# One pool for the weight buffers, stores issued by ScalarE, and later bias-table and cache loads in a streaming-encoder kernel

## Chip, cores and metric

The kernel runs on one core of one Trainium2 chip. The metric is device time in microseconds (us) of one execution; lower is better. The engines are called PE (TensorE matmul), PEld (its weight load), DVE (VectorE), ACT (ScalarE), POOL (GpSimd) and SP (SyncE); SPq and POOLq are the instruction queues of SP and POOL from which DMAs are issued.

## What is computed

One layer for 640 tokens (512 of a prompt, 128 new ones of eight streams), as five tiles of 128 tokens, width 2048. In short form:

```
z            = rmsnorm(x) @ w_in                   # q, k, v, u, vs, ga, gb
h            = sigmoid(ga) * (attention(q, k, v) @ w_pa)
             + sigmoid(gb) * (sgu(u, rmsnorm(gelu(vs))) @ w_pb)
x            = x + h @ w_out
q            = rmsnorm(x) @ w_query                # 8 heads, two half keys each
pick 16 of the 128*128 experts per head: scores sv, indices eidx, g = softmax(scores)
a            = gelu(expert_u[eidx] . rmsnorm(x))
y            = rmsnorm(x + sum((g * a) * expert_v[eidx]))
```

Attention is a sliding window with a bias table (`rel_bias_table`, by bucket of the distance) and, for the sampled tile, cached keys and values. Inputs and outputs are fp32.

## The kernel before

**Matrix products.** Every large product goes through `gemm` (L192). For two steps of 128 along the contraction it loads one `raw` tile (512 KB, L198); for each step ACT casts it to `whi` (fp32r, L143) and DVE makes the remainder `wlo` (L144; every `pl`-th one goes to POOL in some stages). For each token tile `i` PE then runs three matmuls, L211, L212 and L213 (whi with xh, wlo with xh, whi with xl), into one `acc` bank. Below, a **k-step** is this group for all token tiles of the stage: nine matmuls where there are three.

**Stages.** Two tiles (0 and the sampled one) go through `prep`, `mix` and `query` first, then the other three (1, 2, 3). For those three, the experts are computed densely (`dense_peer`, L802): `U` runs twelve gemms of x with the expert rows ("U loop", about 1750 to 2206 us in the trace), then sixteen rounds of `V` and the later `U` follow ("d stage", to the end). For tiles 0 and SAMPLE, single expert rows are gathered in the background (L754, used by DVE at L740 and L745).

**Weights of the experts.** Alongside the U loop, `weights` (L774) builds for each of the three tiles a matrix `wd` in DRAM in 32 steps: DVE and ACT make one-hot tiles `s` (L789, L795; ACT L792, L793), PE multiplies them (L796), ACT copies the result out of PSUM (L798), SP stores 256 KB (L799). `h_step` (L807) loads `wd` back into a `b` tile (L99), DVE multiplies it with the activation (L814), PE transposes it (L818), and ACT and DVE split it into `HT`, which `V` uses as its left side. `late(s)` is an `h_step` whose activation `ad` was stored by `U` (L831) and is loaded again. `late(0)` and `late(1)` are queued while the U loop still runs; each handles the three tiles one after the other.

**Order.** The side work sits in a list of generators (`side`), of which `gemm` runs one step every so often (`pump`). From this the Tile framework makes a fixed order of instructions for each engine; an engine runs its own list strictly in order, and waits on semaphores. SP issues nearly all loads and stores.

**Buffers.** The pools `wk` (work tiles: `s`, `S`, `e`, `b`) and `st` (`raw`, `whi`, `wlo`) are opened by `open_work`. After the U loop `work.close()` closes both, and they are opened again with other counts for the d stage (L863 to L868):

```python
                work.close()
                cfg.update(s=12, S=D_STAGE, b=D_LOAD, raw=D_RAW, w=D_W)
                open_work("d")
```

`whi` and `wlo` have N_W = 5 buffers each up to there and D_W = 6 in the d stage; `raw` has 4 in both, `b` 4 in both. A tile of the new pools waits for the old tiles that lay in its memory.

**Start.** `bias_table` (L219) multiplies the bias table with a one-hot matrix (L228) and stores the product 32 times over (768 KB) to DRAM as `bvd` (L231); it is the first generator in `side`. `start` is the generator that loads and splits the first two tiles' x (L426). `sample_consts` (L312) loads the caches.

Of the kernel before, what the change touches and what calls it, by code (L numbers as in the profile page):

```python
# [37 lines left out]
N_LOAD = 4  # L38
N_STAGE = 6
N_W = 5  # L40
D_W = 6
D_RAW = 4
D_STAGE = 5
D_LOAD = 4
N_RAW = 4
# [14 lines left out]
def body(tc, A, O):  # L60
    nc = tc.nc
    with ExitStack() as ctx:
# [6 lines left out]

        cfg = dict(s=N_SLOT, e=N_EV, b=N_LOAD, S=N_STAGE, raw=N_RAW, w=N_W)  # L70
        work = ExitStack()
        pools = {}

        def open_work(name):
            pools["wk"] = work.enter_context(tc.tile_pool(name="wk" + name, bufs=1, reuse_waits="tile"))
            pools["st"] = work.enter_context(tc.tile_pool(name="st" + name, bufs=1, reuse_waits="tile"))

        open_work("a")
        uid = [0]

        def nm(s):
            uid[0] += 1
            return f"{s}_{uid[0]}"

        def mtile(shape, dt=F32):
            return mt.tile(shape, dt, name=nm("m"), tag="m")

        def slot(shape=(128, 512), dt=F32):
            return pools["wk"].tile(list(shape), dt, name=nm("s"), tag="s", bufs=cfg["s"])

        def stage(shape=(128, 512), dt=F32):
            return pools["wk"].tile(list(shape), dt, name=nm("S"), tag="S", bufs=cfg["S"])

        def evs(shape=(128, 512)):
            return pools["wk"].tile(list(shape), F32, name=nm("e"), tag="e", bufs=cfg["e"])
# [9 lines left out]
        def misc(shape=(128, 512)):  # L105
            return pm.tile(list(shape), F32, name=nm("pm"), tag="pm")
# [23 lines left out]
        def stat(w=1):  # L130
            nstat[0] += w
            assert nstat[0] <= 208
            return stats[:, nstat[0] - w:nstat[0]]
# [41 lines left out]
        side = []  # L175
# [46 lines left out]
        def bias_table():  # L222
            tab = evs((32, 16))
            nc.sync.dma_start(tab, A["table"])
            oh = evs((32, 384))
            nc.sync.dma_start(oh, A["onehot"])
            p = misc()
            nc.tensor.matmul(p[:16, :384], tab, oh, start=True, stop=True)  # L228
            bv = evs((16, 384))
            nc.vector.tensor_copy(bv, p[:16, :384])  # L230
            nc.sync.dma_start(bvd, bv.unsqueeze(1).to_broadcast([16, 32, 384]))  # L231
            for _ in range(5):
                yield


# [76 lines left out]
        def sample_consts(vnat, out):  # L312
            vnd = dr.tile([128, 128], F32, name="vnd")
            nc.sync.dma_start(vnd, vnat)
            yield
            kc = mtile([128, 2, 8, 128])
            nc.vector.memset(kc, 0.0)
            for kv in range(2):
                nc.sync.dma_start(kc[kv * 64:kv * 64 + 64, kv], A["kcT"][kv * 64:kv * 64 + 64])
            vc = mtile([128, 8, 128])  # L320
            nc.sync.dma_start(vc, A["vc"])
            sk = stat(2)
            nc.sync.dma_start(sk, A["sinks_s"])
            bias = slot((128, 2, 144))
            for kv in range(2):
                nc.sync.dma_start(bias[:, kv, :],
                                  bass.AP(tensor=bvd.tensor, offset=bvd.offset + kv * 8 * 32 * 384 + 127,
                                          ap=[[32 * 384, 8], [383, 16], [1, 144]]))
            vn = mtile([16, 8, 128])
            nc.sync.dma_start(vn, vnd.rearrange("(b t) d -> t b d", b=8))  # L330
            out.extend((kc, vc, vn, sk, bias))
            yield

# [439 lines left out]
        wd = {}  # L773

        def weights(ti, ijg):
            wd[ti] = dr.tile([128, 16384], F32, name=nm("wd"))
            pt = misc((128, 4, 128))
            for c in range(3):
                nc.tensor.transpose(pt[:, c, :], ijg[:, c, :], ident)
            tr = stage((128, 4, 128))  # L780
            nc.scalar.copy(tr[:, 0:3, :], pt[:, 0:3, :])
            nc.vector.tensor_scalar_mul(tr[:, 3, :], tr[:, 1, :], -1.0)  # L782
            for t0 in range(0, 128, 4):
                pw = misc((128, 4, 128))
                for t in range(t0, t0 + 4):
                    if t % 2 == 0:
                        ab = slot((128, 4, 128))
                    a, b = ab[:, t % 2 * 2, :], ab[:, t % 2 * 2 + 1, :]
                    nc.vector.tensor_scalar(a, io128, tr[:, 0, t:t + 1], tr[:, 2, t:t + 1],  # L789
                                            op0=ALU.is_equal, op1=ALU.mult)  # L790
                    if t % 4 < ACT_OH:
                        nc.scalar.activation(b, io128, AF.Abs, bias=tr[:, 3, t:t + 1])  # L792
                        nc.scalar.activation(b, b, AF.Relu, bias=1.0, scale=-1.0)  # L793
                    else:
                        nc.vector.tensor_scalar(b, io128, tr[:, 1, t:t + 1], None, op0=ALU.is_equal)  # L795
                    nc.tensor.matmul(pw[:, t - t0, :], a, b, start=True, stop=True)  # L796
                w = slot((128, 4, 128))
                nc.scalar.copy(w, pw)  # L798
                nc.sync.dma_start(wd[ti][t0:t0 + 4, :].rearrange("t (i j) -> i t j", i=128), w)  # L799
                yield  # L800

        def dense_peer(G, x2T, r2, x1d):  # L802
            n = len(G)
            ad = [[dr.tile([128, 512], F32, name=nm("ad")) for _ in G] for _ in range(LEAD)]
            if True:
# [17 lines left out]
                def abuf():  # L823
                    return stage()

                def U(s, ticks):
                    def ev(i, ps):
                        a = abuf()
                        nc.scalar.activation(a, ps, AF.Gelu_apprx_tanh, scale=r2[i])
                        if s < LEAD:  # L830
                            nc.sync.dma_start(ad[s][i], a)  # L831
                        else:
                            side.append(h_step(s, i, a))
                    gemm(x2T, 0, KC, A["UT"][s], ev, ticks)
# [29 lines left out]
                drain()  # L864
                pl[0] = 0
                work.close()
                cfg.update(s=12, S=D_STAGE, b=D_LOAD, raw=D_RAW, w=D_W)
                open_work("d")  # L868
                steps[0] = 1.0
                for b in range(16):  # L870
# [3 lines left out]
                    for nb in range(4):  # L874
                        s = 2 * b + 2 + nb // 2
# [9 lines left out]
                for c in range(4):  # L885
                    cs = slice(c * 512, c * 512 + 512)
                    for i, ti in enumerate(G):
                        t = y[i, c]
# [8 lines left out]
        start = prep(G1, x1a, r1a, [(i, c) for c in range(4) for i in range(2)])  # L897
        next(start)
        next(start)
        side.append(bias_table())  # L900

        def start_rows(kc):
            if kc % 2 == 0 and kc:
                next(start)
                next(start)
            if kc == 6:
                side.insert(0, start)

        nextg = prep(G2, x1b, r1b, [(i, c) for i in range(3) for c in range(4)])

# [103 lines left out]
```

## Time and profile before

| what | value |
|---|---|
| median of 3 runs | 3988.98 us (3987.25 to 3996.61) |
| profiled execution, its own time | 3996.57 us |
| span of the profiled execution | 3994.9 us |
| PE busy | 3883.8 us, 97% of the span |
| DVE busy | 3153.5 us, 79% |
| ACT busy | 1728.2 us, 43% |
| POOL busy | 829.1 us, 21% |
| mean DMA rate | 296 GB/s |

The span is the time from the first to the last instruction in the trace; the execution's own time is 1.67 us longer. Busy time of an engine leaves out DMA-issuing instructions and waits. The granted clock is TensorE's, as a share of its full level.

### The profile page before, as it was taken

The numbers are of one execution on the slowest core, as the hardware profiler recorded it, in microseconds if no ns is written. First come the engines' busy times: TensorE is split into PE (matmuls) and PEld (weight loads), VectorE is DVE, ScalarE is ACT, GpSimd is POOL, SyncE is SP. The second block draws the span as 40 slices with busy tenths as digits, with TensorE's granted clock in tenths as the row PEclk, the third lists the DMA queues.
The fourth block names the chain that finished last, engine by engine and source line by source line (L and its number), as shares of the span: only waits on it lengthen the run. The fifth ranks groups of instructions, "written<-read, shape, count | busy, mean of one in ns | idle before, by whom it ended". The sixth has DMA issues, their size and how long they took to land. (4 is left out here: it accounts for less than half of the span.)

```text
span 3994.9 us, 52665 instructions
## 1 busy us (share of the span) xinstructions
PE 3883.8 (97%) x17880; PEld 3177.5 (80%) x17880; DVE 3153.5 (79%) x5421; ACT 1728.2 (43%) x3338; POOL 829.1 (21%) x678
## 2 busy tenths in 40 slices
PE   8999998999999999999999899999999999999998
PEld 6778786877777888877878788877888888888886
DVE  4655769966767987899977688878888888888888
ACT  5665554444444334436665333333333333333333
POOL 1000113211212223211111112222222222222222
PEclk9999999999999999999999999999999999999999
DMA  7666786777878997569988989989998999999987
GB/s 224 204 187 208 248 264 201 273 276 279 311 277 286 336 334 249 206 198 314 327 264 288 338 325 338 342 299 365 338 350 336 353 331 345 345 340 349 346 337 290
DMA packets 333919, 1180.51 MB, mean 296 GB/s; under 512 B 35840, under 2 KB 94784, under 8 KB 267088
## 3 DMA queue, kind: packets, MB, share of 16 engines
q1 hardware_dynamic: 259824, 640.15, 47.9%
q0 software_dynamic: 73824, 536.99, 35.0%
q8 instruction: 141, 2.31, 0.2%
q14 instruction: 130, 1.06, 0.1%
HBM read 1117.69 MB, written 59.31 MB: 295 GB/s over the span
## 5 line engine op out<-in xcount | busy, mean ns | idle before, releaser
L211 PE MATMUL acc<-whi,m 128*128 128x512 f32 (+1 forms) x5232 | 2066.7, 395 | 23.3 <-ACT whi L143 18.3
L212 PE MATMUL acc<-wlo,m 128*128 128x512 f32 (+1 forms) x5232 | 2049.8, 392 | 22.5 <-DVE wlo L144 22.4
L213 PE MATMUL acc<-whi,m 128*128 128x512 f32 (+1 forms) x5232 | 2044.1, 391 | 0.3 <-DVE m L144 0.2
L143 ACT CAST whi<-raw 128x512 fp32r<-128x512 f32 (+1 forms) x1888 | 1157.9, 617 | 1979.3 <-PE acc L213 1646.6
L144 DVE TENSOR_TENSOR wlo<-raw,whi 128x512 fp32r<-128x512 f32 (+1 forms) x1824 | 1221.5, 689 | 526.8 <-ACT whi L143 523.1
L212 PEld LDWEIGHTS acc<-wlo,m 128*128 128x128 f32 x5232 | 990.7, 189 | 227.1 <-DVE wlo L144 34.5
L211 PEld LDWEIGHTS acc<-whi,m 128*128 128x128 f32 x5232 | 989.3, 189 | 225.4 <-ACT whi L143 20.6
L213 PEld LDWEIGHTS acc<-whi,m 128*128 128x128 f32 x5232 | 989.5, 189 | 202.7 <-DVE m L144 0.8
L740 DVE SCALAR_TENSOR_TENSOR gb<-gb,xa 128x2048 f32<-128x2048 f32 x256 | 589.6, 2303 | 79.5 <-DMA gb<-in_U,idx 69.1
L745 DVE SCALAR_TENSOR_TENSOR xa<-gb,hw,xa 128x2048 f32<-128x2048 f32 x239 | 560.3, 2344 | 70.4 <-DMA gb<-in_V,idx 64.1
L754 POOL DMA_INDIRECT gb<-in_V,idx x239 | 318.5, 1333 | 1228.8 <-DVE wlo L144 331.2
L754 POOL DMA_INDIRECT gb<-in_U,idx x256 | 339.6, 1327 | 1018.9 <-ACT whi L143 366.2
L144 POOL TENSOR_TENSOR wlo<-raw,whi 128x512 fp32r<-128x512 f32 x64 | 91.5, 1431 | 261.8 <-ACT whi L143 229.7
L796 PEld LDWEIGHTS pm<-s 128*128 128x128 f32 x768 | 102.6, 193 | 30.5 <-ACT s L793 14.6
L796 PE MATMUL pm<-s 128*128 128x128 f32 x768 | 113.7, 283 | 10.0 <-DVE s L789 8.0
L789 DVE TENSOR_SCALAR s<-io,S 128x128 f32<-128x128 f32 x384 | 114.8, 339 | 3.6 <-DMA wd<-s 3.6
L847 DVE TENSOR_TENSOR s<-s,acc 128x512 f32<-128x512 f32 x180 | 112.5, 678 | 0.0
L144 DVE TENSOR_TENSOR m<-pm,m 128x512 fp32r<-128x512 f32 (+1 forms) x142 | 93.5, 661 | 7.5 <-ACT m L143 6.5
L143 ACT CAST m<-pm 128x512 fp32r<-128x512 f32 (+1 forms) x142 | 79.6, 563 | 16.3 <-PE pm L362 6.3
L798 ACT COPY s<-pm 128x512 f32<-128x512 f32 x96 | 56.5, 588 | 64.8 <-PE pm L796 64.2
L814 DVE TENSOR_TENSOR b<-b,b 128x512 f32<-128x512 f32 x36 | 24.8, 688 | 56.0 <-DMA b<-wd 53.5
L792 ACT ACTIVATE s<-io,S 128x128 f32<-128x128 f32 x192 | 66.7, 398 | 3.6 <-DVE S L782 2.3
(194 smaller groups left out, 1668.7 us busy)
## 6 DMA issues: line engine op xcount, KB each, us to landing
raw<-in_UT SPq DMA_DIRECT2D x256, 512.0 KB, 6.2
raw<-in_VP SPq DMA_DIRECT2D x256, 512.0 KB, 6.5
raw<-in_w_in SPq DMA_DIRECT2D x224, 512.0 KB, 4.6
raw<-in_w_out SPq DMA_DIRECT2D x64, 512.0 KB, 5.4
raw<-in_w_q SPq DMA_DIRECT2D x64, 512.0 KB, 4.5
wd<-s SPq DMA_DIRECT2D x96, 256.0 KB, 6.0
b<-wd SPq DMA_DIRECT2D x96, 256.0 KB, 5.2
raw<-in_w_pa SPq DMA_DIRECT2D x32, 512.0 KB, 4.2
```

The costliest lines, as they stand in the source:

```text
L143: mark[0] = nc.scalar.copy(hi, src).ins
L144: (E or nc.vector).tensor_sub(lo, src, hi.bitcast(F32))
L211: nc.tensor.matmul(o, xh, hi, start=(k == 0), stop=False)
L212: nc.tensor.matmul(o, xh, lo, start=False, stop=False)
L213: nc.tensor.matmul(o, xl, hi, start=False, stop=(k == K - 1))
L740: q = nc.vector.scalar_tensor_tensor(t, t, 1.0, xg, op0=ALU.mult, op1=ALU.mult, accum_out=dots[:, j:j + 1])
L745: q = nc.vector.scalar_tensor_tensor(y, t, hw[:, j:j + 1], y, op0=ALU.mult, op1=ALU.add)
L754: d = nc.gpsimd.indirect_dma_start(out=t, out_offset=None, in_=src, in_offset=bass.IndirectOffsetOnAxis(ap=idx[j // 32][:, j % 32:j % 32 + ...
L789: nc.vector.tensor_scalar(a, io128, tr[:, 0, t:t + 1], tr[:, 2, t:t + 1], op0=ALU.is_equal, op1=ALU.mult)
L792: nc.scalar.activation(b, io128, AF.Abs, bias=tr[:, 3, t:t + 1])
L796: nc.tensor.matmul(pw[:, t - t0, :], a, b, start=True, stop=True)
L847: nc.vector.tensor_add(y[i, nb], x1, ps)
```

## The change

1. The pool `st` is opened once and is never closed; `D_W` and `D_RAW` go, so `whi` and `wlo` keep 5 buffers in the d stage. `wk` is closed and opened again as before.
2. The stores of `wd` (96 of them) and of `ad` (36) are issued by ScalarE (`nc.scalar`) instead of SyncE.
3. `bias_table` yields three times instead of five, and goes into `side` behind `start` once the first gemm is at its seventh `raw`, instead of first of all.
4. In `sample_consts` the loads of `vn` and `sk` come first, the memset of `kc` goes from DVE to GpSimd, and a yield stands behind each load of the caches.

```diff
 N_W = 5
-D_W = 6
-D_RAW = 4
...
-        pools = {}
+        pools = {"st": ctx.enter_context(tc.tile_pool(name="st", bufs=1))}
 
         def open_work(name):
             pools["wk"] = work.enter_context(tc.tile_pool(name="wk" + name, bufs=1, reuse_waits="tile"))
-            pools["st"] = work.enter_context(tc.tile_pool(name="st" + name, bufs=1, reuse_waits="tile"))
...
             nc.sync.dma_start(bvd, bv.unsqueeze(1).to_broadcast([16, 32, 384]))
-            for _ in range(5):
+            for _ in range(3):
                 yield
...
+            vn = mtile([16, 8, 128])
+            nc.sync.dma_start(vn, vnd.rearrange("(b t) d -> t b d", b=8))
+            sk = stat(2)
+            nc.sync.dma_start(sk, A["sinks_s"])
             kc = mtile([128, 2, 8, 128])
-            nc.vector.memset(kc, 0.0)
+            nc.gpsimd.memset(kc, 0.0)
             for kv in range(2):
                 nc.sync.dma_start(kc[kv * 64:kv * 64 + 64, kv], A["kcT"][kv * 64:kv * 64 + 64])
+                yield
             vc = mtile([128, 8, 128])
             nc.sync.dma_start(vc, A["vc"])
-            sk = stat(2)
-            nc.sync.dma_start(sk, A["sinks_s"])
+            yield
             bias = slot((128, 2, 144))
...
-            vn = mtile([16, 8, 128])
-            nc.sync.dma_start(vn, vnd.rearrange("(b t) d -> t b d", b=8))
             out.extend((kc, vc, vn, sk, bias))
...
-                nc.sync.dma_start(wd[ti][t0:t0 + 4, :].rearrange("t (i j) -> i t j", i=128), w)
+                nc.scalar.dma_start(wd[ti][t0:t0 + 4, :].rearrange("t (i j) -> i t j", i=128), w)
...
                         if s < LEAD:
-                            nc.sync.dma_start(ad[s][i], a)
+                            nc.scalar.dma_start(ad[s][i], a)
...
-                cfg.update(s=12, S=D_STAGE, b=D_LOAD, raw=D_RAW, w=D_W)
+                cfg.update(s=12, S=D_STAGE, b=D_LOAD)
...
-        side.append(bias_table())
...
             if kc == 6:
-                side.insert(0, start)
+                side.extend([start, bias_table()])
```

The lists of instructions move with it. Line numbers of the changed kernel are 1 to 3 lower: its L208, L209 and L210 are the three matmuls of a k-step, L795 is the product of the one-hots, L813 the multiply of `b`, L817 the transposes.

**PE around the end of the U loop.** `acc_19976` and `acc_20419` are banks of its last k-steps, `raw_20671` is its last load. Before, the last product of `weights` (`pm_20266`) lies 24 k-steps ahead of the loop's end (the rows at its place, amid the loop):

```order
L212 MATMUL acc_19976<-wlo_20254,m_12743 128x512
L213 MATMUL acc_19976<-whi_20253,m_12744 128x512
L796 MATMUL pm_20266<-s_20267 128x128 x2
L796 MATMUL pm_20266<-s_20276 128x128 x2
L211 MATMUL acc_19974<-whi_20288,m_12739 128x512
L212 MATMUL acc_19974<-wlo_20289,m_12739 128x512
```

In the changed kernel:

```order
L209 MATMUL acc_20419<-wlo_20687,m_12743 128x512
L210 MATMUL acc_20419<-whi_20686,m_12744 128x512
L795 MATMUL pm_20215<-s_20216 128x128
L795 MATMUL pm_20215<-s_20225 128x128 x2
L795 MATMUL pm_20266<-s_20267 128x128
L817 MATMUL pm_20320<-ident,b_20317 128x128 x4
L795 MATMUL pm_20266<-s_20267 128x128
L795 MATMUL pm_20266<-s_20276 128x128 x2
L208 MATMUL acc_20715<-whi_20720,m_20316 128x512
L209 MATMUL acc_20715<-wlo_20721,m_20316 128x512
L817 MATMUL pm_20395<-ident,b_20361 128x128 x4
```

The last product of `weights` now comes behind the U loop's last matmul (`acc_20419<-whi_20686`) and just ahead of the first matmul of `V` (`acc_20715`); the transposes of the first tiles of `late(1)` have moved there too. 20 matmuls of `V` further on, PE has the transposes of the third tile, `b_20405`.

**SP around the end of the U loop.** `raw_20671` is the loop's last load, `in_VP` is V's weight matrix, `wd_19046` belongs to the third token tile. Before:

```order
L198 DMA raw_20671<-in_UT 128x1024
L831 DMA ad_15264<-S_20702 128x512
L831 DMA ad_15265<-S_20705 128x512
L831 DMA ad_15266<-S_20708 128x512
L198 DMA raw_20722<-in_VP 128x1024
L99 DMA b_20750<-ad_15237 128x512
L99 DMA b_20753<-wd_16498 128x512
L198 DMA raw_20759<-in_VP 128x1024
L198 DMA raw_20794<-in_VP 128x1024
```

In the changed kernel:

```order
L195 DMA raw_20671<-in_UT 128x1024
L195 DMA raw_20718<-in_VP 128x1024
L195 DMA raw_20755<-in_VP 128x1024
L195 DMA raw_20790<-in_VP 128x1024
L195 DMA raw_20827<-in_VP 128x1024
L195 DMA raw_20880<-in_VP 128x1024
L96 DMA b_20405<-wd_19046 128x512
L96 DMA b_20455<-ad_15234 128x512
L96 DMA b_20457<-wd_16498 128x512
```

The loads of V's weights no longer stand behind the stores of `ad`, and the load of `b_20405`, which was amid the U loop, now comes behind five of them.

**DVE where `late(1)` takes its first tile.** `s_17728` is the last one-hot tile of the first token tile, `b_20317` the first part of its finished matrix `wd`, loaded back. Before, 31 rows lie between them (24 of them left out here):

```order
L795 TENSOR_SCALAR s_17728<-io_82,S_16503 128x128
L144 TENSOR_TENSOR wlo_17833<-raw_17817,whi_17832 128x512
L745 SCALAR_TENSOR_TENSOR xa_14811<-gb_17548,hw_14808,xa_14811 128x2048
L144 TENSOR_TENSOR wlo_17871<-raw_17868,whi_17870 128x512
L144 TENSOR_TENSOR wlo_17884<-raw_17868,whi_17883 128x512
L745 SCALAR_TENSOR_TENSOR xa_14811<-gb_17687,hw_14808,xa_14811 128x2048
L782 TENSOR_SCALAR S_17771<-S_17771 128x128
...
L144 TENSOR_TENSOR wlo_18035<-raw_18019,whi_18034 128x512
L814 TENSOR_TENSOR b_20317<-b_20317,b_20314 128x512
```

In the changed kernel 13 rows lie between them, eight of them left out here, all one-hots:

```order
L794 TENSOR_SCALAR s_17728<-io_82,S_16503 128x128
L141 TENSOR_TENSOR wlo_18083<-raw_18067,whi_18082 128x512
L781 TENSOR_SCALAR S_17771<-S_17771 128x128
L744 SCALAR_TENSOR_TENSOR xa_14811<-gb_17865,hw_14808,xa_14811 128x2048
L788 TENSOR_SCALAR s_17775<-io_82,S_17771 128x128 x2
...
L794 TENSOR_SCALAR s_17804<-io_82,S_17771 128x128
L813 TENSOR_TENSOR b_20317<-b_20317,b_20314 128x512
L141 TENSOR_TENSOR wlo_18141<-raw_18138,whi_18140 128x512
```

The multiply of `b_20317` has moved up towards the one-hots whose product it uses, and stands ahead of the next `wlo`.

## Rows read from the trace of the kernel before

Times are us from the span's start; in brackets stands the idle time of the engine just before, and what ended it.

**Rows 1.** The windows view of three stretches of 100 us. Columns: stretch, its length, then busy time (and instructions) of PE, PEld, DVE, ACT and POOL, the granted TensorE clock, the DMA engines' busy share, GB/s.

```profile
0.00:100.00 100.00, 80.74 (x360) 65.81 (x361) 49.65 (x94) 54.43 (x117) 11.96 (x24) 0.93 0.77 224
2000.00:2100.00 100.00, 91.89 (x485) 76.64 (x484) 78.04 (x198) 61.09 (x164) 14.01 (x10) 0.95 0.83 271
3000.00:3100.00 100.00, 100.00 (x454) 82.75 (x454) 84.35 (x110) 36.06 (x60) 24.30 (x18) 1.00 0.91 340
```

**Rows 2.** The same view of the start, in stretches of 5 us.

```profile
5.00:10.00 5.00, 2.40 (x5) 0.88 (x6) 3.59 (x7) 2.77 (x7) 2.57 (x2) 1.00 0.95 339
10.00:15.00 5.00, 5.00 (x25) 5.00 (x25) 3.96 (x8) 2.41 (x5) 1.28 (x2) 1.00 0.62 98
...
20.00:25.00 5.00, 1.83 (x7) 1.54 (x8) 1.82 (x4) 2.16 (x5) 2.03 (x2) 0.74 0.99 299
```

**Rows 3.** The timeline of the start: the store of the bias table on SP and what PE waited for. The second row is that store in the list of DMA issues (size, us from issue to landing).

```profile
10.88 0.70 SPq L231 DMA_DIRECT2D bvd<-e  x1
...
bvd<-e SPq DMA_DIRECT2D x1, 768.0 KB, 9.7
...
23.07 0.58 PE L211 MATMUL acc<-whi,m 128*128 128x256 f32 x1 [5.02 <-ACT m L143]
...
52.40 0.49 PE L211 MATMUL acc<-whi,m 128*128 128x512 f32 x1 [3.59 <-ACT whi L143]
```

**Rows 4.** The timeline where the last store of a `wd` and the first load that needs all of it meet, for the second token tile: DVE's last one-hot, SP's stores (two, of which the second is issued at the end of the 4.23 us) and its load, DVE's multiply and PE behind it; then the windows row of the ten us that follow.

```profile
2031.92 0.28 DVE L795 TENSOR_SCALAR s<-io,S 128x128 f32<-128x128 f32 x1
2030.93 4.23 SPq L799 DMA_DIRECT2D wd<-s  x2
2043.18 0.33 SPq L99 DMA_DIRECT2D b<-wd  x1
2049.20 0.69 DVE L814 TENSOR_TENSOR b<-b,b 128x512 f32<-128x512 f32 x1 [8.68 <-DMA b<-wd]
2050.89 0.55 PE L796 MATMUL pm<-s 128*128 128x128 f32 x1 [8.03 <-DVE s L789]
2050.00:2060.00 10.00, 9.11 (x37) 7.84 (x38) 8.30 (x22) 4.28 (x12) 0.00 (x0) 0.67 0.43 115
```

**Rows 5.** The same meeting for the first token tile: DVE's last one-hot, the last store, the first load behind it, and DVE's multiply.

```profile
1919.26 0.28 DVE L795 TENSOR_SCALAR s<-io,S 128x128 f32<-128x128 f32 x1
1920.73 0.58 SPq L799 DMA_DIRECT2D wd<-s  x1
1928.18 0.33 SPq L99 DMA_DIRECT2D b<-wd  x1
1936.27 0.67 DVE L814 TENSOR_TENSOR b<-b,b 128x512 f32<-128x512 f32 x1
```

**Rows 6.** DMA issues of the stretch 1800 to 2210 us (count, KB each, median us from issue to landing), and the tile view of `wd` in 2020 to 2060 us.

```profile
wd<-s SPq DMA_DIRECT2D x96, 256.0 KB, 6.0
b<-wd SPq DMA_DIRECT2D x7, 256.0 KB, 5.3
...
DMA to landing us min/median/max: 2.3/4.2/6.9
```

**Rows 7.** The end of the U loop: SP's waits for ACT at the store of `ad` (from the list of waits: us in total, times, longest), the timeline of ACT, SP and PE, and the windows row.

```profile
SPq L831 <- ACT S L829: 54.6, 29, 20.2
...
2204.66 2.05 ACT L829 ACTIVATE S<-acc,stats 128x512 f32<-128x512 f32 x3 [8.22 <-PE acc L213]
2205.38 1.68 SPq L831 DMA_DIRECT2D ad<-S  x3
2207.22 0.34 SPq L198 DMA_DIRECT2D raw<-in_VP  x1
2212.34 0.80 PE L211 MATMUL acc<-whi,m 128*128 128x512 f32 x1 [6.37 <-ACT whi L143]
2212.00:2218.00 6.00, 5.66 (x14) 4.21 (x15) 5.68 (x7) 3.09 (x6) 2.11 (x2) 0.57 1.04 417
```

**Rows 8.** The last store of `wd` in the kernel before.

```profile
2158.84 0.36 SPq L799 DMA_DIRECT2D wd<-s  x1
```

**Rows 9.** The d stage (2210 to 3990 us): three entries of its list of waits (us in total, times, longest), the first of each of three groups of PE's stalls, ACT's casts in steady state, and DVE at a gathered row.

```profile
ACT whi L143 <- PE acc L213: 996.3, 712, 3.9
DVE xa L745 <- DMA gb<-in_V,idx: 64.1, 41, 5.0
PE acc L212 <- DVE wlo L144: 8.5, 7, 2.6
...
2681.19 0.69 PE L212 MATMUL acc<-wlo,m 128*128 128x512 f32 x1 [1.90 <-DVE wlo L144]
2732.26 0.50 PE L212 MATMUL acc<-wlo,m 128*128 128x512 f32 x1 [1.38 <-DVE wlo L144]
3348.11 0.50 PE L212 MATMUL acc<-wlo,m 128*128 128x512 f32 x1 [1.09 <-DVE wlo L144]
3525.30 0.62 ACT L143 CAST whi<-raw 128x512 fp32r<-128x512 f32 x1 [1.42 <-PE acc L213]
3527.34 0.62 ACT L143 CAST whi<-raw 128x512 fp32r<-128x512 f32 x1 [1.42 <-PE acc L213]
```

**Rows 10.** The windows row of the U loop, and one store of `wd` on SP.

```profile
1800.00:2206.00 406.00, 391.55 (x2064) 326.61 (x2064) 347.81 (x787) 253.74 (x655) 58.30 (x48) 0.98 0.89 298
2089.94 0.37 SPq L799 DMA_DIRECT2D wd<-s  x1
```

## The prediction

> **What bounds the kernel now.** I read the windows view first. At 3000 us PE is busy throughout at granted clock 1.00, at 2000 us it is busy for 91.89 of 100 us, in the first 100 us for 80.74 [rows 1]. PE sets the pace, so nothing on DVE, ACT, POOL or SP counts unless PE runs out of work, and the change moves no matmul out of the program. I then went through the gaps between PE's instructions. Four kinds lie where the diff acts: the start, the meeting of the stores and loads of `wd`, the end of the U loop, and a few short ones in the d stage. [...] So a gap is priced with its clock: (1 - 0.67) x 9.11 busy us = 3.0 on top of the 8.03, (1 - 0.57) x 5.66 = 2.4 on top of the 6.37.
>
> **Unit.** A matmul of 512 columns leaves PE every 0.227 us, as ACT's casts show, which follow each other in 2.04 us = nine matmuls [rows 9].
>
> **The change part by part.** The sum is made against the profiled execution, 3996.57 us; the median of the runs is 7.6 us lower, and the forecast is given against the median.
>
> *1. Bias table.* The store of `bvd`, 768 KB, is issued at 10.88 and lands 9.7 us later; while it runs the DMAs move 98 GB/s, against 339 before it and 299 after [rows 2, 3]. The loads of x stand behind it, and PE waits 5.02 us at 23.07 and 3.59 us at 52.40 [rows 3]. In the changed order the store comes among the loads of the first query product. The 5.02 and its clock, (1 - 0.74) x 1.83 = 0.5 in the row up to 25 us [rows 2] and more behind it, some 8 in all, can go. Against that, the product with the table stands in PE's list in the fifth k-step of the query product, right behind its own loads, a wait of about 2 us, and the three `raw` behind the store take the slow transfer: up to the same 8. The nearest rows thus give -11 (both gaps with part of their clock) to +3. I take **-5**, as the store has `raw` buffers ahead of it in the new place and only x's loads in the old.
>
> *2. Caches, memset.* The loads are the same, some earlier, and the memset leaves DVE, which is busy for 49.65 of the first 100 us [rows 1]. PE waits for none of them. **0**; without that cover it would be one memset, under 1 us.
>
> *3. Stores on ACT, issue time.* 132 stores at 0.37 us, SP's price [rows 10], are 49 us of ACT's time, spread over the U loop, where ACT is busy 253.74 of 406 us [rows 10]. Cover: its idle 152 us. **0**; the case that it delays the casts is a rival.
>
> *4. The meeting of stores and loads, second tile.* Before: last one-hot at 2031.92, last store at about 2034.8, load issued 2043.18, DVE idle 8.68 us until 2049.20, PE idle 8.03 us, with the clock 11.0 [rows 4]. In the changed order DVE has about as many rows between (6.3 us of them, 7.4 before), so this stays: **0**, bounds -3 to +1.
>
> *5. The same, first tile.* Before, DVE's multiply comes at 1936.27, 17.0 us behind the last one-hot, and did not wait [rows 5]: 31 rows lay between. Now 13 do: one `wlo` at 0.68, one row of the gathers at 2.35, twelve one-hots at about 0.3 and one small row, together 7 us. From the last one-hot to the data took 17.3 us at the second tile (2031.92 to 2049.20) [rows 4]. DVE would stand at the multiply for some 10 us, with `wlo` behind it. PE holds about 9.6 us of k-steps beyond that one-hot; with 1.7 us from the multiply to PE's next input (2049.20 to 2050.89) its gap is 17.3 + 1.7 - 9.6 = 9.4 at the most. With a store and a load of 6.0 and 5.3 [rows 6] in place of the 8.3 and 6.0 there, it is 6.4. Landings scatter from 2.3 to 6.9 [rows 6], so I take 5.5 with 2.5 of clock: **+8**, bounds 0 (short landings) to +11 (as the second tile).
>
> *6. End of the U loop.* SP stood 20.2 us at a store of `ad`, waiting for ACT's activation, with V's first weights behind it; PE's gap is 6.37 and its clock 2.4: **8.8** that go, since SP now issues five `raw` of V ahead of anything that waits for late work. What is late next: before, `weights` had ended at 2158.84, 47 us before the loop's end [rows 8]. Now its last product is PE's last work of the loop. From there (T0), one-hots and ACT's activations of `ad` (2.05 for three [rows 7]) and copy bring the last store to about T0 + 5.5; store and load, 6.0 and 5.3 [rows 6], bring `b_20405` to T0 + 17; PE has 20 matmuls of V (4.5 us) and two sets of transposes before it needs that tile. So it loses 11 to 12, then one to two stalls while the next tiles come through the same four `b` buffers, in all 14 to 16, with 2 to 4 of clock. Net 15 + 3 - 8.8 = **+9**, bounds -9 (the new chain is hidden) to +16 (loads of the next three tiles to T0 + 25).
>
> *7. Five instead of six `whi`/`wlo` in the d stage.* ACT's casts wait 712 times for PE to free a buffer [rows 9]: the buffers set how far ahead ACT and DVE run, and one less is 2.04 us less. DVE waits up to 5.0 us for a gathered row [rows 9], with `wlo` behind it. PE already waited seven times, 8.5 us, in three groups, which begin at 2681, 2732 and 3348 [rows 9]. If each group grows by the lost 2.04: **+6**. Bounds 0 (they grow only where the lead was used up) and +13 (six of the seven by 2.04). Reopening `st` cost its waits at the end of the U loop alone, priced in 6.
>
> Sum: -5 + 0 + 0 + 0 + 8 + 9 + 6 = +18, that is 4014.6 against the profiled execution and **4007 us** against the median. The forecast's own range is 3996 to 4020.
>
> **Queues and the hardware page.** The row on which part 6 begins shows a queue that is held by a wait: SP stands at the store for 20.2 us, while its issue takes 0.37 [rows 7, 10]. The Trainium skill ("DMA: Bandwidth & Descriptors", section "Issuing engines are not separate DMA queues") says that DMAs begun by the scalar, sync or gpsimd engine run on the same 16 DMA engines, and that issuing from several saves only the sequencer's time, usually small. By that rule moving the stores would change nothing, and the time would be that of the second rival below. The row speaks against it, as a wait and not an issue is taken off SP.
>
> **Rivals.**
> - *Faster: landings are short.* The store of `wd` no longer queues behind SP's loads. At each meeting 5.9 us of PE's cover are left for store and load together (9.6 less 3.0 from one-hot to store and 0.7 for the multiply); where they take less (the shortest store seen is 2.3 [rows 6]), the meetings cost nothing. Then the second tile's 11 goes, the first adds 0, the U loop's end gives -3, start -5, d stage +6: -13, about 3976. Against it: 6.0 and 5.3 are medians of this stretch [rows 6], and the second tile took 8.3 and 6.0. Chance 0.13.
> - *No change: only start and d stage act.* New waits at the meetings and at the U loop's end come out as large as the 8.8 that goes, or DVE runs later relative to PE than its list suggests, so that the load is there in time: -5 + 6 = +1, about 3990. For it: at the first tile before, the load was in time though issued 7 us behind the store [rows 5]. Chance 0.27.
> - *Slower still: ACT binds in the U loop.* A store in ACT's list must wait for its copy and for a free DMA slot; casts stand behind it. If that costs one k-step, 2.04 us, in each of twelve gemms, 24 come on top: about 4031. It decides once ACT waits longer than the lead of `whi`, four k-steps. Against it: ACT's idle share [rows 10]. Chance 0.10.
>
> **How the numbers follow.** The forecast has 0.50. The runs tell a difference of 0.3%, 12 us, from none, so "same" is 3977 to 4001. Of the forecast's 0.50, 0.37 lies above 4001 and 0.13 within; of the second rival's 0.27, 0.20 is within, 0.04 above, 0.03 below; the fast rival gives 0.08 below and 0.05 within; the slow one 0.10 above. Faster 0.11, same 0.38, slower 0.51. The range reaches from the fast rival's 3976 to 4030, just short of the slow one's: it leaves out half of each and the forecast's far ends, some 0.17.
>
> **What would show it.** In the changed profile: PE's wait for x near 23 us gone, and one at the table's product (L225) near 40; in the list of waits the multiply L813 waiting for the load of `wd` with over 5 us in one piece a second time, near 1940 to 1970; at the U loop's end no wait of PE for `raw` through ACT, but 10 us or more at L817, released by DVE L813 and that by the load of `wd`; in the d stage PE's waits at L209 for `wlo` at 12 us or more in sum, in place of 8.5. ACT's waits for a copy or slot ahead of its stores should not show up at PE. The forecast is wrong if the U loop's end costs less than 6 us, if the first meeting shows no stall, or if PE's stalls in the d stage don't grow; each takes its term out of the sum. A shorter time than 3977 would need the second tile's stall gone.

## The result, and the profile of the changed kernel

| | before | changed |
|---|---|---|
| median of 5 runs | 3988.14 us (3987.25 to 3996.61) | 4027.67 us (4013.92 to 4036.61) |
| profiled execution, its own time | 3996.57 us | 4028.55 us |
| its span | 3994.9 us | 4026.9 us |

The changed kernel is slower: ratio 1.0092, 95% interval 1.0075 to 1.0109, that is 37 us (30 to 43). The execution profiled of the kernel before is 8.4 us above its median, which matters below. Of E7 and E8 below, one execution each, of 7888.57 and 10287.69 us, is slow and left out of the ratio.

The start, by the windows view (columns as in [rows 1]), and by the timeline of PE and SP, answering to [rows 2, 3]; the store's line of the DMA issues stands last:

```profile
0.00:100.00 100.00, 82.58 (x374) 66.76 (x375) 51.55 (x96) 55.28 (x120) 15.10 (x25) 0.93 0.79 227
10.00:15.00 5.00, 4.35 (x25) 3.55 (x24) 5.00 (x6) 2.85 (x7) 4.34 (x5) 1.00 0.95 268
...
16.67 0.39 PE L209 MATMUL acc<-wlo,m 128*128 128x256 f32 x1 [2.01 <-DVE wlo L141]
27.55 0.73 PE L208 MATMUL acc<-whi,m 128*128 128x512 f32 x2 [1.25 <-ACT whi L140]
32.43 1.22 PE L208 MATMUL acc<-whi,m 128*128 128x512 f32 x2 [2.96 <-ACT whi L140]
42.31 0.69 SPq L228 DMA_DIRECT2D bvd<-e  x1
54.52 0.50 PE L208 MATMUL acc<-whi,m 128*128 128x512 f32 x1 [2.85 <-ACT whi L140]
...
bvd<-e SPq DMA_DIRECT2D x1, 768.0 KB, 9.7
```

The store of the bias table has gone from 10.88 to 42.31 us and takes its 9.7 us there. The DMAs move 268 GB/s at 10 to 15 us, not 98; the gap of 5.02 us is gone, that of 3.59 is now 2.85, and three others add 6.2.

The two meetings of stores and loads of `wd` (timeline of DVE and PE), answering to [rows 5] and [rows 4]:

```profile
1943.92 0.69 DVE L813 TENSOR_TENSOR b<-b,b 128x512 f32<-128x512 f32 x1 [6.79 <-DMA b<-wd]
1945.62 0.46 PE L795 MATMUL pm<-s 128*128 128x128 f32 x2 [2.03 <-DVE s L788]
...
2075.35 0.69 DVE L813 TENSOR_TENSOR b<-b,b 128x512 f32<-128x512 f32 x1 [7.49 <-DMA b<-wd]
2076.45 0.46 PE L795 MATMUL pm<-s 128*128 128x128 f32 x2 [0.50 <-DVE s L788]
```

DVE now stands at both, 6.79 and 7.49 us; PE loses 2.03 and 0.50.

The end of the U loop: the timeline of SP, ACT's queue, DVE and PE, answering to [rows 7]:

```profile
2163.20 0.33 SPq L195 DMA_DIRECT2D raw<-in_VP  x1
...
2174.89 0.33 SPq L195 DMA_DIRECT2D raw<-in_VP  x1
...
2195.53 0.38 ACTq L798 DMA_DIRECT2D wd<-s  x1
2202.50 0.33 SPq L96 DMA_DIRECT2D b<-wd  x1
2207.03 0.69 DVE L813 TENSOR_TENSOR b<-b,b 128x512 f32<-128x512 f32 x1 [5.42 <-DMA b<-wd]
...
2200.46 0.50 PE L210 MATMUL acc<-whi,m 128*128 128x512 f32 x1 [2.30 <-DVE m L141]
2207.87 1.09 PE L817 MATMUL pm<-ident,b 128*128 128x128 f32 x4 [5.30 <-DVE b L813]
2219.30 0.68 PE L817 MATMUL pm<-ident,b 128*128 128x128 f32 x4 [2.72 <-DVE b L813]
2243.69 1.09 PE L817 MATMUL pm<-ident,b 128*128 128x128 f32 x4 [4.86 <-DVE b L813]
2297.17 0.50 PE L209 MATMUL acc<-wlo,m 128*128 128x512 f32 x1 [2.32 <-DVE wlo L141]
2302.93 1.09 PE L817 MATMUL pm<-ident,b 128*128 128x128 f32 x4 [2.84 <-DVE b L813]
2323.49 0.50 PE L209 MATMUL acc<-wlo,m 128*128 128x512 f32 x1 [2.28 <-DVE wlo L141]
```

V's first weights are loaded from 2163.20 on (2174.89 is the third of five loads), and PE no longer waits for them. It waits for `b`: the last store of `wd` at 2195.53, its load at 2202.50, the multiply at 2207.03, the transposes at 2207.87. The first four gaps make 15.2 us, the three behind them 7.4.

The d stage: PE's entry in the list of waits from 2200 us on, against 8.5 in 7 waits [rows 9], and the windows row of a stretch early in it, here for the changed kernel:

```profile
PE acc L209 <- DVE wlo L141: 26.4, 21, 2.9
...
2310.00:2490.00 180.00, 169.07 (x756) 136.16 (x754) 141.66 (x161) 54.93 (x92) 40.50 (x27) 0.99 0.87 313
```

and for the kernel before, where PE has no idle time in the same stretch:

```profile
2310.00:2490.00 180.00, 180.00 (x825) 148.91 (x825) 156.80 (x182) 60.11 (x100) 36.09 (x28) 1.00 0.91 334
```

**Where the 32 us between the two profiled executions lie.** PE's idle time makes 17 us of them (111.1 to 127.8). The other 15 are its busy time, 3883.8 and 3899.1 us for the same 17,880 matmuls, at a mean granted clock of 0.990 before and 0.987 now. Both run the same 15,696 large matmuls, nearly all in the same order, so the start of the nth can be compared. In us, difference to the profiled execution of before, by stretch; the kernels E1 to E12 are those of the next section.

| stretch (us in before) | changed | E1 | E2 | E3 | E4 | E7 | E9 | E12 |
|---|---|---|---|---|---|---|---|---|
| to 68 | -2.7 | +0.1 | +2.1 | -4.0 | -4.3 | -3.5 | -0.4 | -0.1 |
| 68 to 1771 | -3.4 | -0.1 | -1.6 | -2.3 | -5.2 | -2.8 | -14.2 | -4.4 |
| U loop, to 2212 | -11.7 | -5.9 | +17.2 | -13.4 | +16.7 | -7.1 | +16.6 | -9.9 |
| V's first rounds, to 2341 | +29.8 | +0.6 | +2.0 | +5.7 | +8.6 | -4.3 | -3.2 | -8.6 |
| 2341 to 2480 | +13.3 | +13.5 | +1.5 | +12.5 | +2.2 | +2.5 | +2.8 | 0.0 |
| 2480 to 2771 | +5.8 | +5.1 | +0.5 | +7.8 | -0.4 | -0.4 | +1.0 | +5.9 |
| 2771 to end | +0.9 | +0.7 | -0.4 | +1.6 | -1.0 | -0.5 | -0.7 | +2.7 |

The -5.9 of E1 and -7.1 of E7, where nothing of the U loop was changed, show that before's profiled execution had an unusually long stall there: its gap of 8.03 us [rows 4] is 3.07 and 2.71 in theirs. E5, E10 and E12, which also run before's U loop, have 2.69, 2.57 and 2.67. The U loop and V's first rounds are best read together, since the changed order moves 20 small matmuls from the one to the other.

### The profile page after: what moved, and what is told of

Read it like the earlier page. It is cut to its first block, busy times and chain, and to the rows that moved or that the text cites. A ratio compares the mean times of both kernels' runs of the same rounds, so it can differ in the third digit from the quotient of the medians.

```text
span 4026.9 us, 52474 instructions
## 1 busy us (share of the span) xinstructions
PE 3899.1 (97%) x17880; PEld 3185.9 (79%) x17880; DVE 3155.2 (78%) x5420; ACT 1739.0 (43%) x3338; POOL 823.7 (20%) x679
## 5 line engine op out<-in xcount | busy, mean ns | idle before, releaser
L209 PE MATMUL acc<-wlo,m 128*128 128x512 f32 (+1 forms) x5232 | 2056.8, 393 | 43.3 <-DVE wlo L141 43.0
L208 PE MATMUL acc<-whi,m 128*128 128x512 f32 (+1 forms) x5232 | 2069.4, 396 | 15.3 <-ACT whi L140 15.3
L210 PE MATMUL acc<-whi,m 128*128 128x512 f32 (+1 forms) x5232 | 2052.4, 392 | 2.6 <-DVE m L141 2.6
L209 PEld LDWEIGHTS acc<-wlo,m 128*128 128x128 f32 x5232 | 992.6, 190 | 255.6 <-DVE wlo L141 62.6
L208 PEld LDWEIGHTS acc<-whi,m 128*128 128x128 f32 x5232 | 990.5, 189 | 217.0 <-ACT whi L140 17.7
L210 PEld LDWEIGHTS acc<-whi,m 128*128 128x128 f32 x5232 | 991.5, 189 | 203.8 <-DVE m L141 3.6
L795 PEld LDWEIGHTS pm<-s 128*128 128x128 f32 x768 | 115.8, 193 | 27.9 <-ACT s L792 10.1
L795 PE MATMUL pm<-s 128*128 128x128 f32 x768 | 120.1, 279 | 7.3 <-ACT s L792 4.3
L813 DVE TENSOR_TENSOR b<-b,b 128x512 f32<-128x512 f32 x36 | 24.9, 692 | 84.8 <-DMA b<-wd 77.2
L791 ACT ACTIVATE s<-io,S 128x128 f32<-128x128 f32 x192 | 75.9, 396 | 5.4 <-DMA wd<-s 3.4
```

What stands on the lines that cost most here:

```text
L208: nc.tensor.matmul(o, xh, hi, start=(k == 0), stop=False)
L209: nc.tensor.matmul(o, xh, lo, start=False, stop=False)
L210: nc.tensor.matmul(o, xl, hi, start=False, stop=(k == K - 1))
```

## Experiments

Each ratio is to the kernel before, on the same chip. Two theories were set against each other. **Buffers:** the lost pair of `whi` and `wlo` costs the d stage its lead. **Late weights:** the stores on ScalarE put the work on `wd` behind the U loop.

**E1, five buffers alone.**

```diff
-D_W = 6
+D_W = 5
```

> Kernel before with one number changed: five whi/wlo in the d stage instead of six; pools are still closed and opened again, all stores on SP. Buffer theory (the lost pair of buffers costs the d stage its lead): 10 to 25 us slower than before, near 4005, with PE's waits for wlo in the d stage up from 8.5 to over 20 us. Late-weights theory (the stores on ACT push the work on wd behind the end of the U loop, and the d stage starts late and stays late): within 5 us of before, near 3989.

Measured: 4004.38 us, ratio 1.0048 (1.0035 to 1.0061): 19 us. The cost lies at 2341 to 2771 us, where the changed kernel has it too. Its list of waits for 2310 to 2490 us, and its timeline at one stall:

```profile
DVE b L814 <- DMA b<-wd: 36.5, 12, 6.2
...
PE acc L212 <- DVE wlo L144: 7.7, 5, 2.9
...
2348.79 0.69 DVE L814 TENSOR_TENSOR b<-b,b 128x512 f32<-128x512 f32 x1 [2.20 <-DMA b<-wd]
2349.39 2.35 DVE L745 SCALAR_TENSOR_TENSOR xa<-gb,hw,xa 128x2048 f32<-128x2048 f32 x1
2351.66 1.29 DVE L144 TENSOR_TENSOR wlo<-raw,whi 128x512 fp32r<-128x512 f32 x2
2352.40 0.50 PE L212 MATMUL acc<-wlo,m 128*128 128x512 f32 x1 [1.87 <-DVE wlo L144]
```

DVE waits for a load of `wd`, then has a gathered row of 2.35 us ahead of the `wlo` that PE needs. Before, DVE waited for these loads too (19.8 us in the stretch), and the lead covered it.

**E2, stores on ScalarE alone.**

```diff
-                nc.sync.dma_start(wd[ti][t0:t0 + 4, :]...
+                nc.scalar.dma_start(wd[ti][t0:t0 + 4, :]...
-                            nc.sync.dma_start(ad[s][i], a)
+                            nc.scalar.dma_start(ad[s][i], a)
```

> Kernel before with the stores of wd and ad on ScalarE and nothing else: six whi/wlo in the d stage. Buffer theory: U loop 11 us shorter, U loop's end 10 to 15 us longer, d stage as before; near 3990. Late-weights theory: 15 to 30 us slower than before, near 4010, lost between the U loop's end and 2350 us at PE's transposes of b, which wait for the load of wd.

Measured: 4018.48 us, ratio 1.0081 (1.0068 to 1.0094): 32 us. In its order PE's last product of `weights` and all six transposes of `late(0)` and `late(1)` come behind the U loop. Its SP's longest wait (2150 to 2260 us), PE's timeline, and ACT's and SP's rows:

```profile
SPq L99 <- DMA wd<-s: 40.2, 3, 25.7
...
2199.04 0.37 ACTq L799 DMA_DIRECT2D wd<-s  x1
2205.29 0.33 SPq L99 DMA_DIRECT2D b<-wd  x1
2212.20 1.09 PE L818 MATMUL pm<-ident,b 128*128 128x128 f32 x4 [12.82 <-DVE b L814]
2218.24 1.09 PE L818 MATMUL pm<-ident,b 128*128 128x128 f32 x4 [3.61 <-DVE b L814]
2222.97 1.09 PE L818 MATMUL pm<-ident,b 128*128 128x128 f32 x4 [3.64 <-DVE b L814]
2229.93 1.65 PE L211 MATMUL acc<-whi,m 128*128 128x512 f32 x3 [5.88 <-ACT whi L143]
```

The chain is the forecast's: SP stands 25.7 us until the last store has landed, 6.3 us behind its issue, with V's weights behind it. PE idles 26 us in these four gaps.

**E3, the changed kernel with the stores back on SP** (the diff of E2 reversed).

> Changed kernel with the stores of wd and ad back on SP: five whi/wlo in one pool, bias table and cache loads as changed. Buffer theory: 10 to 20 us slower than before, near 4003, nearly all of it at PE's waits for wlo after 2217 us. Late-weights theory: 3 to 8 us faster than before, near 3983 (the start's gain, and V's first weights in time).

Measured: 3999.36 us, ratio 1.0041 (1.0029 to 1.0052): 16 us. Five buffers (+0.48%) and the new start (-0.15%, E7) make +0.33%; so the open pool adds or saves nothing that can be told. Why it saves nothing at the U loop's end: PE no longer waits 6.37 us for V's weights, but nearly as long for `b`:

```profile
2208.23 1.09 PE L817 MATMUL pm<-ident,b 128*128 128x128 f32 x4 [5.88 <-DVE b L813]
```

**E4, the changed kernel with `st` reopened and six buffers.**

```diff
-        pools = {"st": ctx.enter_context(tc.tile_pool(name="st", bufs=1))}
+        pools = {}
...
+            pools["st"] = work.enter_context(tc.tile_pool(name="st" + name, bufs=1, reuse_waits="tile"))
...
-                cfg.update(s=12, S=D_STAGE, b=D_LOAD)
+                cfg.update(s=12, S=D_STAGE, b=D_LOAD, raw=N_RAW, w=6)
```

> Changed kernel with the pool of raw, whi and wlo closed and opened again as before, six whi/wlo in the d stage; stores on ScalarE, bias table and cache loads as changed. Buffer theory: 20 to 30 us faster than the changed kernel, near 4000. Late-weights theory: within 10 us of the changed kernel, near 4020.

Measured: 4013.86 us, ratio 1.0067 (1.0054 to 1.008). Against the changed kernel's 1.0092 that is some 10 us, at the edge of the second expectation and short of the first: the table gives the buffers' share at 2341 to 2771 back (+1.8 in place of +19.1), but U loop and V's first rounds are 7 us longer than in the changed kernel. There PE begins V at 2194.49 while `b` is on its way; here it begins at 2219.77, behind the transposes. So five buffers (19) and the stores (32) do not simply add up.

**E5, five buffers and six `b` tiles** (`D_W = 5`, `D_LOAD = 6`).

> Kernel before with five whi/wlo in the d stage and six b tiles instead of four (the memory of the lost pair goes to b, so that the loads of wd and ad can start two tiles earlier). If the lost pair costs time because DVE stands at the multiply of wd, waiting for its load, with wlo behind it: most of the 19 us that five whi/wlo cost alone go, near 3990, and DVE's waits for the load of wd between 2310 and 2490 us fall from 36.5 us to under 15. If the lead is lost to something else (gathered rows, ACT's casts): still near 4004.

Measured: 4010.74 us, ratio 1.0063 (1.0049 to 1.0077), no faster than E1. DVE's waits for these loads stay at 32.3 us in the stretch: six tiles did not make SP issue the loads earlier (from a load's issue to its multiply the median is 6.6 us, in E1 7.4, in before 6.5). The edit did not remove what it was to remove, and decides nothing.

**E6, stores on ScalarE, side work of the U loop called more often** (E2 with `SW = 2.0` in place of 1.6).

> Kernel before with the stores of wd and ad on ScalarE, and the side work of the U loop called a quarter more often (SW 2.0 instead of 1.6), which puts the last product of weights 19 k-steps ahead of the U loop's end again (22 before, none with the stores on ScalarE alone). If the late weights are what the stores on ScalarE cost: the 32 us go but for some 5, near 3990, and PE has no wait over 3 us at its transposes of b near the U loop's end. If stores on ScalarE cost time by themselves (casts held behind them, slower landings): still near 4010.

Measured: 4041.16 us, ratio 1.0132 (1.0116 to 1.0147). The late-weights theory fails as the whole story. `weights` ends 19 k-steps ahead of the loop's end here, and yet PE has a gap of 12.50 us. It is not a clean test: PE still waits 5.44 and 3.11 us at transposes of `b`, of which the first come 11 us behind the last store of `wd`. From the list of SP's waits (2190 to 2262 us) and the timeline:

```profile
SPq L99 <- DMA ad<-S: 15.9, 1, 15.9
...
2229.91 0.33 ACTq L831 DMA_DIRECT2D ad<-S  x1
2231.00 1.20 ACTq L831 DMA_DIRECT2D ad<-S  x2
2238.84 0.33 SPq L99 DMA_DIRECT2D b<-ad  x1
2240.23 0.33 SPq L198 DMA_DIRECT2D raw<-in_VP  x1
2245.96 0.80 PE L212 MATMUL acc<-wlo,m 128*128 128x512 f32 x1 [12.50 <-DVE wlo L144]
```

SP's load of a `b` tile waits until ACT's stores of `ad` have landed, 7 to 9 us behind their issue, and V's weights stand behind it. Before, SP stood at the store itself; with the store on ACT, it stands at the next load.

**E7, bias table, memset and cache loads alone** (parts 3 and 4 of the change).

> Kernel before with the bias table, memset and cache loads as in the changed kernel, and nothing else: six whi/wlo, pools closed and opened again, stores on SP. Both theories: 3 to 6 us faster than before (the changed kernel's matmuls run 2.7 us ahead at 55 us of the trace and 6.1 at 1754), near 3981. If the start's gain is given back in a later stage: within 2 us of before.

Measured: 3983.5 us, ratio 0.9985 (0.9971 to 0.9998): 6 us faster (1 to 12).

**E8, E7 with the stores of `ad` on ScalarE.**

> The same with the stores of ad on ScalarE too, those of wd on SP: the parts of the change that look harmless or good. If the wait of 20.2 us at the store of ad on SP cost the 6.37 us gap at the U loop's end: 6 to 9 us faster than the kernel with the bias table alone, near 3974. If reopening the pool holds V's first weights in any case: no faster than it.

Measured: 3982.45 us, ratio 0.9986 (0.9977 to 0.9995), the same as E7. The gap at V's first matmul falls from 6.50 us to 2.17, but one of 2.47 us at `b` follows it. E7 and E8 are the only versions tried that beat both kernels.

**E9, fewer calls of the side work, stores on SP** (`SW = 1.4`): the order of PE at the U loop's end becomes that of E2, with SP issuing.

> Kernel before, stores on SP, with the side work of the U loop called an eighth less often (SW 1.4 instead of 1.6). In the order this alone puts the last product of weights, and all six transposes of late(0) and late(1), behind the U loop's last matmul, as the stores on ScalarE do. If work on wd that comes last is what costs, whoever issues the stores: 20 to 32 us slower than before, near 4013, PE waiting some 20 us in all at transposes of b near the U loop's end. If it takes the stores on ScalarE for that: within 8 us of before.

Measured: 4001.32 us, ratio 1.0036 (1.0022 to 1.0051): 14 us, between the expectations. PE waits 8.9 us at those transposes, not 20. In the table, 13 of the -14.2 us ahead of the loop come back by 1800 us: a wait of 7 us lies ahead of the border at 1771 us before, and behind it here. The first line is of the kernel before, the rest is E9's:

```profile
1763.80 0.87 PE L779 MATMUL pm<-ident,S 128*128 128x128 f32 x3 [7.08 <-DVE S L676]
...
1771.90 0.87 PE L779 MATMUL pm<-ident,S 128*128 128x128 f32 x3 [7.34 <-DVE S L676]
...
2196.06 0.36 SPq L799 DMA_DIRECT2D wd<-s  x1
2198.46 0.33 SPq L99 DMA_DIRECT2D b<-wd  x1
2201.49 0.69 DVE L814 TENSOR_TENSOR b<-b,b 128x512 f32<-128x512 f32 x1 [2.94 <-DMA b<-wd]
```

Counted from 1800 to 2341 us, behind that wait, E9 takes 12 us longer than E7, whose U loop is unchanged, and E2 takes 31. So late work on `wd` with SP issuing costs less than half of what E2 loses at that place. The chain itself is shorter here: 5.4 us from the last store's issue to the multiply, 12.3 in E2. From 2195 to 2205 us the DMA engines' busy share is 0.47 here and 0.74 in E2, where gathered rows are loaded just then. Whether the stores' queue or the order made that so is not shown, and the slower pace of the side work is part of E9 too.

**E10, five buffers, multiply freed from the loads.** E1, with the multiply in `h_step` as follows (it leaves out the weights, so its outputs are not the layer's):

```diff
-                    nc.vector.tensor_mul(w, w, a)
+                    if s > 1 and s < LEAD:
+                        w = stage()
+                        idb = ident.unsqueeze(1).to_broadcast([128, 4, 128])
+                        nc.vector.tensor_mul(w.rearrange("p (g t) -> p g t", g=4), idb, idb)
+                    else:
+                        nc.vector.tensor_mul(w, w, a)
```

> Kernel before with five whi/wlo in the d stage, where the multiply of late(2) to late(11) takes a resident tile (the identity, squared) in place of the loaded wd and ad. The loads are still made, but nothing waits for them; the products are not the weights'. If five buffers cost time through DVE's waits for the load of wd: PE idle between 2330 and 2470 us under 2 us instead of 7.9, and 10 to 15 us faster than five buffers alone, near 3992. If the time is lost to the gathered rows or to the casts: near 4004 with PE idle there as before.

Measured: 4015.9 us, ratio 1.0073 (1.0057 to 1.0088). Slower, and not the clean test it was meant to be. ACT and SP in 2310 to 2490 us, from the list of waits:

```profile
ACT whi L143 <- DMA raw<-in_VP: 50.1, 9, 9.8
...
SPq L99 <- DMA b<-wd: 20.0, 11, 6.0
```

Since nothing reads the `b` tiles, SP waits for the earlier load into the same tile, and `raw` comes late in its place. Freeing DVE alone moved the wait.

**E11, stores of `wd` on GpSimd** (`nc.gpsimd.dma_start` for them, else before).

> Kernel before with the stores of wd issued by GpSimd; the order of PE stays that of before (weights end 22 k-steps ahead of the U loop's end). If taking stores off SP is worth something by itself: 4 us or more faster than before. If SP's issue and waits are covered: within 5 us. If a store that waits in another engine's list holds that engine's own work: POOL's gathers stand behind it, DVE waits longer for gathered rows in 1770 to 2160 us, and the time is 5 to 20 us longer.

Measured: 3986.84 us, ratio 1.0003 (0.9994 to 1.0011): no difference. PE's order stays that of before (the last product of `weights` 22 k-steps ahead of the loop's end, in either trace). Taking 96 stores off SP is worth nothing.

**E12, five buffers without the loads of `wd` and `ad` in `late(2)` to `late(11)`.** E10's multiply, and `a = load(ad[s][i]) if s < 2 else None`, `w` not loaded (the weights are left out here too).

> Kernel before with five whi/wlo in the d stage and without the loads of wd and ad in late(2) to late(11) (60 loads of 256 KB); their multiply takes a resident tile, so the products are not the weights'. If the fifth pair's loss shows because these loads come late, to DVE or through SP and the shared DMA engines to raw: PE idle between 2330 and 2470 us under 2 us, and near 3988. If gathered rows and the loads of V alone already use up the lead of five: idle near 8 us there and near 4003.

Measured: 3987.56 us, ratio 1.0003 (0.9992 to 1.0013), 18 us below E1. The windows row, and PE's waits from 2480 to 2771 us, first here, then before:

```profile
2310.00:2490.00 180.00, 180.00 (x824) 148.92 (x823) 153.58 (x176) 59.94 (x100) 34.93 (x28) 1.00 0.81 283
...
PE acc L212 <- DVE wlo L144: 12.9, 9, 3.0
...
PE acc L212 <- DVE wlo L144: 6.6, 4, 2.6
```

PE idles no more in the first stretch, with five buffers. So what the sixth pair covered at 2341 to 2480 us is these sixty loads. The whole time does not say that five buffers are free without them. From 2480 to 2771 us E12 is 5.9 us longer than before, as E1 is 5.1. V's first rounds, where no load of `b` holds PE any more, are 8.6 shorter, and six buffers without the loads were not run. Whether the sixty loads act by DVE's wait for them, SP's, or the DMA engines they share with `raw` (share 0.81 here, 0.91 in before), E10 left open.

## Why the prediction was right, and where its steps were off

Forecast 4007 us, slower, range 3976 to 4030; measured 4027.67. The direction and the forecast's mechanisms stand, the size is about twice the +18. That the time lies inside the range is in part luck: it is above the forecast's own 3996 to 4020, and the range went up to 4030 for the rival in which ACT binds, which did not come.

- **Start, -5.** Right: E7 gives -6. The wait at the table's product, one of its costs, did not come.
- **Memset and caches, 0.** Measured with the start in E7; nothing contrary.
- **Stores' issue time on ACT, 0.** Right as far as the issue goes (0.37 us each, as on SP). PE's waits for `whi` in the whole run fell, 18.3 to 15.3 us, so ACT did not become the bound, as the third rival had it.
- **First meeting, +8.** The wait came, DVE 6.79 us (some 10 forecast, 7.3 by the medians: 3.0 + 6.0 + 5.3 - 7), but PE lost only 2.03, with a clock of 0.66 over the next five us some 3.7. The step that failed is PE's cover: DVE stopped at 1937.1 and PE ran on to 1943.6, 6.5 us; "9.6 us of k-steps beyond that one-hot" less the 7 us of DVE's rows had left 2.6.
- **Second meeting, 0.** Its stall went instead of staying: PE lost 0.50. But 8.03 was that execution's scatter; E1, E5, E10 and E12, the same program up to there, show 3.07, 2.69, 2.57 and 2.67. One profiled execution was too little to price it by.
- **U loop's end, +9.** The chain is right in kind: stores, load, multiply, transposes, four gaps of 15.2 us (14 to 16 forecast), and V's weights come in time. What failed is the rest of the term: three more gaps of 7.4 us come behind, and the lower clock costs more than the 0.6 us (3 - 2.4) that it was put at. Against E7, the U loop and V's first rounds are 29.5 us longer ((-11.7 + 29.8) - (-7.1 - 4.3) in the table), of which E1, with five buffers alone, has 6.1; forecast were 17 with the first meeting. Over the matmuls from 2150 to 2341 us, PE is idle 17.4 us more than in E7, and the clock, as (1 - clock) x busy time in windows of 5 us, costs 6.5 more; E1 has 2.2 and 2.5 of these. E3 shows that V's weights in time are not worth 8.8 by themselves: it has them, and waits 5.88 us for `b` in place of 6.37 for `raw`.
- **Five buffers, +6.** The term that was most mis-sized: 19 us (14 to 24) in E1. The mechanism, a lead shorter by one k-step, is borne out. The old stalls from 2681 us on [rows 9] did grow, in the size forecast: 2480 to 2771 us is 5.1 us longer in E1 and 5.8 in the changed kernel. What failed is the stretch to 2480, priced at nothing because PE never idled there before; it costs 13.5. There the lead was just enough for the loads of `wd` (E12; in E7, with six buffers, PE waits 1.9 us there). A stretch without stalls was read as one without risk. The bound of +13 is a slip too: six times 2.04 is 12.2.

Two terms too small (buffers by 13, U loop's end by some 11), one too large (first meeting by some 4): the sum came out 19 to 21 us low.

**On the clock.** The price of a gap's clock came from two gaps, of 8.03 and 6.37 us [rows 4, 7]. In the same profile the granted clock over the next five us is 0.66 behind the gap of 3.59 at 52.40, but 1.00 behind those of 2.01 at 692.99 and 2.26 at 1641.11, so gaps of about two us do not all cost clock.

**On the queues.** The Trainium skill ("DMA: Bandwidth & Descriptors", section "Issuing engines are not separate DMA queues") would have moving the stores save only issue time. E11 agrees: on GpSimd, 1.0003. E2 does not: on ScalarE, 1.0081, with the same 0.37 us per issue. What its trace shows is a changed order of the engines and SP standing at its next loads, up to 25.7 us. How much of the 32 us is the late weights (E9: 12 of E2's 31 in that stretch), how much the longer landings, and how much the rest (E6 loses more with early weights) stays open; E6 and E9 change the pace of the side work too.

**On the no-change rival** (0.27): it expected the new waits to be no larger than the 8.8 that goes. The gap for V's weights closed in E3 and the changed kernel and shrank to 2.17 in E8, but in each a wait for `b` stood behind it.

## What to carry to other kernels

Before crediting a removed wait, look for what PE needs next at the same place, and when that is ready. A buffer that sets how far the feeding engines run ahead should be priced where the engines behind it wait often, even if PE shows no stall there: those waits are what the lead pays for. And a DMA moved to another engine's queue can move the order around it (E2; not in E11); compare the orders at the stage's end. Price a store-to-load chain by its landings, not by the issue: medians of 6 and 5 us here, but 2.3 and 3 in E9, where the DMA engines had less to do.

## What was not expected of the hardware

The same gap in the same program (second meeting) was 8.03 us in one execution and 2.6 to 3.1 in four kernels that are the same up to there (E1, E5, E10, E12). From the load's issue to the multiply it took 6.0 us in the one, 2.8 in E1 and E5. A store followed by a dependent load took 11.5 us from the store's issue to DVE's multiply in the changed kernel (2195.53 to 2207.03) and 12.3 in E2 (2199.04 to 2211.36), against 14.4 in before at the second meeting and 5.4 in E9.
